# The gate and up projections of a feed-forward stage, with seven products of half blocks in the place of eight

## The chip, the cores and the metric

The kernel runs on one core of one Trainium2 chip. The metric is the time of one execution on the device in microseconds; the time before is the median of three runs. TensorE (PE) multiplies matrices; its weight loads are listed apart as PEld. VectorE (DVE), ScalarE (ACT) and GpSimd (POOL) work element by element, and SyncE (SP) issues the transfers.

## The reference

A decoder trunk of two layers on 512 tokens of width 1024, in float32. The first layer mixes with a gated linear recurrence, the second with RWKV-7; each is followed by the same feed-forward block, and that is what the change touches:

```python
def _conv_ffn(x, norm, w_up, conv_w, conv_b, w_down):
    h = _rmsnorm(x, norm)
    u = jnp.einsum('btd,df->btf', h, w_up)                      # 1024 -> 2 * 3072
    gate = _causal_dwconv(u[..., :D_FF], conv_w, conv_b)        # 3 taps along the tokens
    hid = jax.nn.gelu(gate, approximate=True) * u[..., D_FF:]
    return jnp.einsum('btf,fd->btd', hid, w_down)               # 3072 -> 1024
```

## The kernel before

Channels lie on the 128 partitions and the 512 tokens along the free dimension. Activations are held as blocks of 128 channels; `D_FF` is 24 such blocks for the gate half of `w_up` and 24 for the up half.

**Three matmuls for a product.** Each float32 operand is split into a high part, rounded to the fast format fp32r, and the rest. `mm3` (L51 to L53) issues three matmuls for one product: high by high, high weight by low activation, low weight by high activation. A weight tile holds 1024 elements per partition; `split` (L90, L93) makes its high part on ACT (`wh`) and its low part on DVE (`wl`). `weights_load` fetches such a tile in one transfer of 512 KB, three tiles ahead, and `weights_split` runs two ahead. All these tiles, and the split inputs `xs`, share one pool of 21 buffers (`b4`).

**The feed-forward stage.** `gate_up(third)` makes eight gate blocks and eight up blocks, four at a time, each a sum over 8 blocks of input channels in one bank of PSUM. A gate block is scaled by the norm's factor `rb` (L581, into `gpad`), convolved over tokens (ACT L584, DVE L586 twice) and put through GELU (ACT L588). An up block is scaled (L592), multiplied by the gate (L593), and split into `hid` (L90, L93). `down(third, hid)` multiplies eight blocks of `hid` with `w_down` and adds the sums to the residual. In layer 0 the weights are stationary and the tokens move (L637 adds); in layer 1 the tokens are stationary (L625 to L627, L630), so that the result lies by tokens. The order is gate and up 0, gate and up 1, down 0, gate and up 2, down 1, down 2.

**What stands ahead.** The stage before ends with a projection whose evacuation (`fin`, L532 in layer 0) adds to the residual `x` and at once makes the split input of the feed-forward stage, block by block: `norm_block` (L284 to L291).

**The order.** A scheduler places the instructions of each engine at build time in the order of the program text, as far as it finds buffers and inputs ready by its own estimate, and puts in the waits. On the chip each engine runs its list strictly in that order.

## Time and profile before

| | |
|---|---|
| three runs | 1317.26, 1319.48, 1319.39 us; median 1319.39 us |
| the profiled execution | 1318.34 us, its span 1316.6 us |
| PE, PEld | 1296.2 us (98%), 1057.5 us (80%) |
| DVE, ACT, POOL | 842.1 us (64%), 609.2 us (46%), 72.5 us (6%) |
| granted TensorE clock | 0.998 |
| HBM | 114.44 MB read, 90 GB/s over the span |

The span is the stretch that the profile covers; the execution is 1.74 us longer. A group of the profile is named by line, engine, operation and tiles, with its busy time, the mean duration of one and the idle time just before. Matmuls are pipelined: a duration is longer than the distance from one start to the next, and that distance is the price of one. The same holds, by some 0.08 us, for DVE.

### The profile page before, as it was taken

Reading aid. Unit: us, or ns where it says so; the run is one execution under the profiler, and the core shown is the slowest. Engines: PE = TensorE matmul, PEld = TensorE weight load, DVE = VectorE, ACT = ScalarE, POOL = GpSimd, SP = SyncE. Lnnn points to the kernel's source line nnn. Section 1 sums busy time; section 2 is a strip of 40 time slices with the busy share of each in tenths; the row PEclk is TensorE's granted clock in tenths of the full one; section 3 lists DMA queues with packets and bytes.
Section 4 is the critical chain, followed back from the end, with each engine's and each line's share of the span. In section 5 each row is a group of like instructions: output and inputs, shape, how many; then the busy total and the mean of one; then the engine's idle time right before and its main releaser. Section 6 shows DMA issues by size and latency. Waiting matters only on the chain.

```text
span 1316.6 us, 20618 instructions
## 1 busy us (share of the span) xinstructions
PE 1296.2 (98%) x8547; PEld 1057.5 (80%) x8547; DVE 842.1 (64%) x1276; ACT 609.2 (46%) x964; POOL 72.5 (6%) x114
## 2 busy tenths in 40 slices
PE   9999999999999999999999999999999999999998
PEld 7877888888888888876678787778888888888886
DVE  5988756555436555587989975777564554365523
ACT  6897544233224423358844567655542332244311
POOL 4000000000000000021001121210000000000000
PEclk9999999999999999999999999999999999999999
DMA  6323333323233443213303112133333222334311
GB/s 194 116 64 97 96 112 96 96 64 96 97 96 96 128 116 109 95 37 95 108 25 97 43 53 83 43 97 96 97 96 96 64 96 96 96 96 128 113 63 64
DMA packets 72126, 120.30 MB, mean 91 GB/s; under 512 B 9498, under 2 KB 21476, under 8 KB 71904
## 3 DMA queue, kind: packets, MB, share of 16 engines
q1 hardware_dynamic: 70672, 117.20, 28.6%
q8 instruction: 67, 1.10, 0.3%
q10 hardware_dynamic: 576, 1.05, 0.2%
q0 software_dynamic: 784, 0.74, 0.2%
q14 instruction: 27, 0.22, 0.1%
HBM read 114.44 MB, written 4.52 MB: 90 GB/s over the span
## 4 chain that ended last, share of the span: by engine, by line
PE 85%; DVE 8%; ACT 5%; issue 1%; DMA 0%; SPq 0%; POOLq 0%; POOL 0%; DVEq 0%; ACTq 0%
PE acc L51 22%; PE acc L53 22%; PE acc L52 21%; PE acc L626 3%; PE acc L625 3%; PE acc L627 3%; DVE X L1053 1%; DVE wl L93 1%; DVE DA L1051 1%; PE s L1171 1%; ACT L483 1%; PE pd L1253 1%; ACT L472 0%; PE py L1264 0%; PE pe L1215 0%
## 5 line engine op out<-in xcount | busy, mean ns | idle before, releaser
L51 PE MATMUL acc<-xs,wh 128*128 128x512 f32 x896 | 350.2, 392 | 0.3 <-ACT wh L90 0.3
L53 PE MATMUL acc<-xs,wl 128*128 128x512 f32 x896 | 348.3, 390 | 1.4 <-DVE wl L93 1.4
L93 DVE TENSOR_TENSOR wl<-raw,wh 128x1024 fp32r<-128x1024 f32 (+1 forms) x201 | 242.8, 1216 | 166.1 <-PE acc L52 94.8
L52 PE MATMUL acc<-xs,wh 128*128 128x512 f32 x896 | 348.8, 389 | 0.0
L90 ACT CAST wh<-raw 128x1024 fp32r<-128x1024 f32 (+1 forms) x201 | 207.9, 1045 | 259.2 <-DVE wl L93 169.8
L53 PEld LDWEIGHTS acc<-xs,wl 128*128 128x128 f32 x896 | 168.2, 188 | 37.7 <-DVE wl L93 2.2
L51 PEld LDWEIGHTS acc<-xs,wh 128*128 128x128 f32 x896 | 168.1, 188 | 35.4 <-ACT wh L90 0.8
L52 PEld LDWEIGHTS acc<-xs,wh 128*128 128x128 f32 x896 | 168.3, 188 | 34.4
L586 DVE SCALAR_TENSOR_TENSOR cv<-gpad,pv,cv 128x512 f32<-128x512 f32 x96 | 71.9, 749 | 22.1 <-ACT cv L584 21.0
L90 ACT CAST hid<-un 128x512 fp32r<-128x512 f32 x48 | 29.8, 620 | 108.6 <-DVE un L593 108.6
L626 PE MATMUL acc<-wh,hid 128*128 128x512 f32 (+1 forms) x200 | 76.8, 384 | 0.0
L625 PE MATMUL acc<-wh,hid 128*128 128x512 f32 (+1 forms) x200 | 76.5, 382 | 0.0
L627 PE MATMUL acc<-wl,hid 128*128 128x512 f32 (+1 forms) x200 | 75.9, 380 | 0.0
L52 PE MATMUL acc<-hid,wh 128*128 128x512 f32 x192 | 75.7, 394 | 0.0
L53 PE MATMUL acc<-hid,wl 128*128 128x512 f32 x192 | 75.6, 394 | 0.0
L51 PE MATMUL acc<-hid,wh 128*128 128x512 f32 x192 | 75.5, 393 | 0.0
L592 DVE TENSOR_TENSOR un<-acc,rb 128x512 f32<-128x512 f32 x48 | 33.1, 689 | 44.3 <-PE acc L53 44.3
L93 DVE TENSOR_TENSOR hid<-un,hid 128x512 fp32r<-128x512 f32 x48 | 33.2, 691 | 31.1 <-ACT hid L90 31.1
L584 ACT ACTIVATE cv<-gpad,pv 128x512 f32<-128x512 f32 x48 | 39.2, 817 | 20.7 <-DVE gpad L581 20.5
L588 ACT ACTIVATE ge<-cv 128x512 f32<-128x512 f32 x48 | 30.1, 627 | 35.9 <-DVE cv L586 35.9
L630 DVE TENSOR_TENSOR xtok<-xtok,acc 128x512 f32<-128x512 f32 (+1 forms) x25 | 16.6, 666 | 45.5 <-PE acc L627 45.5
L625 PEld LDWEIGHTS acc<-wh,hid 128*128 128x128 f32 x200 | 37.5, 188 | 8.0
(424 smaller groups left out, 2165.8 us busy)
## 6 DMA issues: line engine op xcount, KB each, us to landing
raw<-in_ffn_w_up_dram SPq DMA_DIRECT2D x96, 512.0 KB, 3.8
raw<-in_ffn_w_down_dram SPq DMA_DIRECT2D x48, 512.0 KB, 3.7
raw<-in_rwkv_w_rkv_dram SPq DMA_DIRECT2D x24, 512.0 KB, 3.9
raw<-in_lru_w_in_dram SPq DMA_DIRECT2D x16, 512.0 KB, 3.9
raw<-in_lru_w_out_dram SPq DMA_DIRECT2D x8, 512.0 KB, 3.9
raw<-in_rwkv_w_out_dram SPq DMA_DIRECT2D x8, 512.0 KB, 3.6
xd<-x SPq DMA_DIRECT2D x8, 256.0 KB, 2.0
AR<-xd SPq DMA_DIRECT2D x1, 2048.0 KB, 7.9
```

The costliest lines, as they stand in the source:

```text
L51: nc.tensor.matmul(ps, wh, xh, start=start, stop=False)
L52: nc.tensor.matmul(ps, wh, xl, start=False, stop=False)
L53: nc.tensor.matmul(ps, wl, xh, start=False, stop=stop)
L90: put = (self.nc.vector.tensor_copy if dve else self.nc.scalar.copy)(hi, src)
L93: self.nc.vector.tensor_tensor(lo, src, hi.bitcast(F32), ALU.subtract)
L584: nc.scalar.activation(cv, gp[:, 0:T], AF.Identity, bias=self.vec(f"ffn_conv_b{l}", fb), scale=cw(0))
L586: nc.vector.scalar_tensor_tensor(cv, gp[:, j : j + T], cw(j), cv, ALU.mult, ALU.add)
L588: nc.scalar.activation(ges[o], cv, AF.Gelu_apprx_tanh)
L592: nc.vector.tensor_tensor(un, ps, rbs[0], ALU.mult)
L625: nc.tensor.matmul(ps, hh[:, s], wh[:, k, m], start=kk == 0, stop=False)
L626: nc.tensor.matmul(ps, hl[:, s], wh[:, k, m], start=False, stop=False)
L627: nc.tensor.matmul(ps, hh[:, s], wl[:, k, m], start=False, stop=kk == 7)
```

## The change

Only the feed-forward stages change. For each pair of blocks the gate half and the up half of `w_up` (1024 rows by 256 columns each) and the input (1024 channels by 512 tokens) are cut in two along the 1024 summed channels; the tokens are cut in two as well. The result is then a two by two matrix of blocks (gate and up, first and last 256 tokens), and seven products of half blocks, each 512 channels deep and 256 tokens wide, stand for eight (Winograd's form of Strassen's way). The price is paid in sums:

- of the inputs, once a stage (`operands`): differences and sums `xt_1479` to `xt_1482`, 12 of them on DVE and 16 splits, 128x256 each; a new `norm_part` makes the first of them while the stage before is evacuated;
- of the weights, once a pair (`Pair.weights`): four sums of 1024 elements per partition on POOL (`S1`, `S2`, `S4`, and one in place), and seven splits where four tiles needed four;
- of the products: three accumulate in a common bank, others are added by DVE or copied by ACT (`s`); the scaling by `rb` moves to POOL for half of the gate and for the finished gate `ge`.

The twelve pairs of a layer are consumed by `down` in four calls of four blocks and one of eight. The order of products is the list `seq`; `ahead` splits weights two products ahead. The number and size of weight transfers stay: 512 KB, 96 for `w_up` and 48 for `w_down`; those of `w_up` now hold four rows of blocks by 256 columns.

```diff
+            def gu(six):
+                for c in range(six * 512, six * 512 + 512, 256):
+                    self.quads.append(len(plan))
+                    for half, r in ((1, 0), (0, 0), (0, 512), (1, 512)):
+                        add(up, r, half * DFF + c, 4, True)
+            def dd(row, n):
                 for g in range(2):
-                    for k in range(0, 8, 2):
-                        add(dn, third * 1024 + k * P, g * 512)
+                    for k in range(0, n, 2):
+                        add(dn, row + k * P, g * 512)
 
             gu(0)
-            gu(1)
-            dd(0)
-            gu(2)
-            dd(1)
-            dd(2)
+            for six in range(1, 6):
+                gu(six)
+                if six < 5:
+                    dd((six - 1) * 512, 4)
+            dd(2048, 8)
...
+    def norm_part(self, b, gain):
+        if b >= KB // 2:
+            return self.norm_block(b, gain)
+        nc = self.nc
+        if b % 2 == 0:
+            self.halves = self.b4(F32R, (2, 2, T // 2), f"xs{b}"), self.b4(F32, (2, 2, T // 2), f"xd{b}")
+        v, d = (t[:, b % 2] for t in self.halves)
+        xb = self.x[:, b, :]
+        nc.scalar.mul(v[:, 0], xb[:, 0 : T // 2], gain)
+        nc.vector.scalar_tensor_tensor(v[:, 1], xb[:, 0 : T // 2], gain, v[:, 0].bitcast(F32), ALU.mult, ALU.subtract)
+        self.squares(b)
+        nc.scalar.mul(d[:, 0], xb[:, T // 2 :], gain)
+        nc.vector.scalar_tensor_tensor(d[:, 1], xb[:, 0 : T // 2], gain, d[:, 0], ALU.mult, ALU.subtract)
+        return v[:, 0], v[:, 1], d[:, 0], d[:, 1]
...
+            def operands():
+                n1, t2, t3, t4 = sums
+                def parts(t, k, f):
+                    nc.scalar.copy(t[:, 0, k], f)
+                    nc.vector.tensor_tensor(t[:, 1, k], f, t[:, 0, k].bitcast(F32), ALU.subtract)
+                for k in range(4):
+                    parts(n1, k, xs[k][3])
+                stt, f = nc.vector.scalar_tensor_tensor, {}
+                for k in range(4):
+                    xb = self.x[:, 4 + k, :]
+                    f[k] = two(t("s", 7))
+                    t2f, t4f = f[k][:, 0], f[k][:, 1]
+                    stt(t2f, xb[:, H:], gain(4 + k), xs[k][3], ALU.mult, ALU.add)
+                    parts(t2, k, t2f)
+                    stt(t4f, xb[:, 0:H], gain(4 + k), t2f, ALU.mult, ALU.subtract)
+                for k in range(4):
+                    if k % 2 == 0:
+                        t3f = two(t("s", 7))
+                    stt(t3f[:, k % 2], self.x[:, 4 + k, H:], gain(4 + k), xs[k][2], ALU.mult, ALU.subtract)
+                    parts(t3, k, t3f[:, k % 2])
+                for k in range(4):
+                    parts(t4, k, f[k][:, 1])
+                op = {1: [xs[k][:2] for k in range(4)]}
+                op[2], op[3] = ([tuple(part[:, h] for part in xs[4 + k]) for k in range(4)] for h in (slice(0, H), slice(H, T)))
+                for i, v in ((5, n1), (6, t2), (7, t3), (4, t4)):
+                    op[i] = [(v[:, 0, k], v[:, 1, k]) for k in range(4)]
+                return op
+            op = operands()
...
+            class Pair:
+                def __init__(pair, n):
+                    i = quads[n]
+                    self.weights_load(i + 4)
+                    pair.n, pair.gp = n, gpads[n % 2]
+                    a11, a21, a22, a12 = (self.loaded.pop(i + j) for j in range(4))
+                    pair.f = {1: a11, 7: a21, 4: a22, 2: a12}
+                    pair.w, pair.bank, pair.s = {}, {}, {}
+                def weights(pair, p):
+                    f = pair.f
+                    if p == 1:
+                        f[5], f[6] = self.b4(F32, (4, 256), "S1"), self.b4(F32, (4, 256), "S2")
+                        gt(f[5], f[7], f[4], ALU.add)
+                        gt(f[6], f[5], f[1], ALU.subtract)
+                        gt(f[7], f[1], f[7], ALU.subtract)
+                    if p == 5:
+                        f[3] = self.b4(F32, (4, 256), "S4")
+                        gt(f[3], f[6], f[2], ALU.subtract)
+                    hi, lo = self.b4(F32R, (4, 256), f"hi{p}"), self.b4(F32R, (4, 256), f"lo{p}")
+                    nc.scalar.copy(hi, f[p])
+                    tt(lo, f[p], hi.bitcast(F32), ALU.subtract)
+                    pair.w[p] = hi, lo
+                def product(pair, p):
+                    name = {1: "A", 5: "F", 2: "D"}.get(p)
+                    if name:
+                        pair.bank[name] = two(self.bank("acc" + name))
+                    ps = pair.bank[name or {3: "F"}.get(p, "A")]
+                    hi, lo = pair.w.pop(p)
+                    for e in range(2):
+                        c = slice(e * P, e * P + P)
+                        for k in range(4):
+                            self.mm3(ps[:, e], (hi[:, k, c], lo[:, k, c]), op[p][k], bool(name) and e + k == 0, e + k == 4, more=not name)
+                        self.background(0.5)
+                    s, bank, gp = pair.s, pair.bank, pair.gp
+                    if p in (1, 6, 7):
+                        s[p] = two(t("s", 7))
+                        nc.scalar.copy(s[p], bank["A"])
+                    if p == 2:
+                        tt(s[1], s[1], bank["D"], ALU.add)
+                    if p == 7:
+                        tt(gp[:, :, 2 + H :], s[7], bank["F"], ALU.subtract)
+                        gt(gp[:, :, 2 + H :], gp[:, :, 2 + H :], rb(H, T), ALU.mult)
+                    if p == 4:
+                        tt(gp[:, :, 2 : 2 + H], bank["A"], rb(0, H), ALU.mult)
+                        pair.gate()
+                    if p == 3:
+                        tt(s[6], s[6], bank["F"], ALU.subtract)
+                        pair.up()
+                def gate(pair):
...
+                    gt(ge, ge, rb(0, T), ALU.mult)
+                def up(pair):
+                    hid = hidden(pair.n)
+                    for i, h in ((1, slice(0, H)), (6, slice(H, T))):
+                        x = pair.s[i]
+                        tt(x, x, pair.ge[:, :, h], ALU.mult)
+                        nc.scalar.copy(hid[:, :, 0, h], x)
+                        tt(hid[:, :, 1, h], x, hid[:, :, 0, h].bitcast(F32), ALU.subtract)
+                    hids.extend((hid[:, e, 0], hid[:, e, 1]) for e in range(2))
...
+            seq = []
+            for n in range(12):
+                if n in (0, 1, 2, 3):
+                    seq += [(n, 1)] + ([(n - 1, 4), (n - 1, 3)] if n else [])
+                elif n % 2:
+                    seq += [(n, 1), (n - 1, 4), (n - 1, 3)]
+                else:
+                    seq += [(n, 1)]
+                seq += [(n, p) for p in (5, 6, 2, 7)]
+                if n % 2 and n > 1:
+                    seq += [(n, 4), (n, 3)]
+            made, at = [0], [0]
+            def ahead(j):
+                while made[0] < min(j, len(seq)):
+                    n, p = seq[made[0]]
+                    if n not in pairs:
+                        pairs[n] = Pair(n)
+                    pairs[n].weights(p)
+                    made[0] += 1
+            def products(upto, more=2):
+                while True:
+                    n, p = seq[at[0]]
+                    at[0] += 1
+                    ahead(at[0] + more)
+                    pairs[n].product(p)
+                    if p == 1 and n < 11:
+                        self.weights_load(quads[n + 1] + 4 if quads[n + 1] == quads[n] + 4 else quads[n] + 6)
+                    if n == 0 and p in (5, 2):
+                        start(int(p == 2))
+                    if p == 7:
+                        self.weights_split(quads[n] + 6)
+                    if (n, p) == upto:
+                        return
...
+            for n in range(3, 12, 2):
+                products((n, 7))
+                if n == 11 and not last:
+                    self.norm_begin()
+                    self.push(self.lora_weights())
+                down(n, 2 * n - 6, 4 if n < 11 else 8, lambda: products((n, 3)), lambda: ahead(at[0] + 2))
```

The lists of the engines change with it. Names ending in a number are tiles of the built program; `raw` is a loaded weight tile, `wh`/`wl` and `hi`/`lo` its high and low parts, `x_68` the residual, and `xd` a part of an input that `norm_part` has made. First DVE, where the stage before layer 0's feed-forward ends (its last evacuation is the first row). Before:

```order
L532 SCALAR_TENSOR_TENSOR x_68<-acc3_1318,pv_78,x_68 128x512
L285 SCALAR_TENSOR_TENSOR xs7_1461<-x_68,pv_78,xs7_1461 128x512
L291 TENSOR_TENSOR sqacc_1144<-sqacc_1144,sq_1464 128x512
L93 TENSOR_TENSOR wl25_1482<-raw25_1385,wh25_1481 128x1024
L93 TENSOR_TENSOR wl26_1521<-raw26_1479,wh26_1520 128x1024
L301 TENSOR_SCALAR ms_1514<-ssq_1509 128x4
L93 TENSOR_TENSOR wl27_1558<-raw27_1518,wh27_1557 128x1024
L93 TENSOR_TENSOR wl28_1564<-raw28_1555,wh28_1563 128x1024
```

Now:

```order
L562 SCALAR_TENSOR_TENSOR x_68<-acc3_1326,pv_78,x_68 128x512
L622 TENSOR_TENSOR xt_1479<-xd0_1255,xt_1479 128x256 x2
L622 TENSOR_TENSOR xt_1479<-xd2_1295,xt_1479 128x256
L293 SCALAR_TENSOR_TENSOR xs7_1465<-x_68,pv_78,xs7_1465 128x512
L304 TENSOR_TENSOR sqacc_1144<-sqacc_1144,sq_1468 128x512
L622 TENSOR_TENSOR xt_1479<-xd2_1295,xt_1479 128x256
L631 SCALAR_TENSOR_TENSOR s_1491<-x_68,pv_78,xd0_1255 128x256
L631 SCALAR_TENSOR_TENSOR s_1496<-x_68,pv_78,xd0_1255 128x256
L633 SCALAR_TENSOR_TENSOR s_1491<-x_68,pv_78,s_1491 128x256
L622 TENSOR_TENSOR xt_1480<-s_1491,xt_1480 128x256
```

And, after fifteen more rows of the same kinds:

```order
L622 TENSOR_TENSOR xt_1482<-s_1506,xt_1482 128x256
L684 TENSOR_TENSOR lo1_1543<-raw24_1387,hi1_1542 128x1024
L684 TENSOR_TENSOR lo5_1549<-S1_1537,hi5_1548 128x1024
L684 TENSOR_TENSOR lo6_1553<-S2_1538,hi6_1552 128x1024
```

Before, the low part that the first product needs (`wl24_1388`) is made ahead of these rows, and the next one stands fourth in them. Now the first, `lo1_1543`, stands behind the 28 operations of `operands` (L622, L631, L633, L637). At the same place PE has, before:

```order
L53 MATMUL acc3_1318<-out_1208,wl23_1382 128x512
L51 MATMUL acc0_1475<-xs0_1254,wh24_1387 128x512
L52 MATMUL acc0_1475<-xs0_1254,wh24_1387 128x512
L53 MATMUL acc0_1475<-xs0_1254,wl24_1388 128x512
L51 MATMUL acc0_1475<-xs1_1271,wh24_1387 128x512
L52 MATMUL acc0_1475<-xs1_1271,wh24_1387 128x512
L53 MATMUL acc0_1475<-xs1_1271,wl24_1388 128x512
```

and now:

```order
L51 MATMUL acc3_1326<-out_1208,wl23_1390 128x512
L51 MATMUL accA_1556<-xs0_1254,hi1_1542 128x256 x2
L51 MATMUL accF_1595<-xt_1479,hi5_1548 128x256
L51 MATMUL accA_1556<-xs0_1254,lo1_1543 128x256
L51 MATMUL accA_1556<-xs0_1254,hi1_1542 128x256 x2
L51 MATMUL accA_1556<-xs0_1254,lo1_1543 128x256
L51 MATMUL accA_1556<-xs2_1294,hi1_1542 128x256 x2
L51 MATMUL accA_1556<-xs2_1294,lo1_1543 128x256
```

The fourth of the new matmuls needs `lo1_1543`, the first weight's low part; what follows it in the list needs it too. Next POOL through the first pairs of layer 0. Before there was nothing there but small work between the stages:

```order
L424 MEMSET graw_484 128x1024
L307 TENSOR_TENSOR rs_1516<-ms_1514,mhalf_76 128x4
L307 TENSOR_TENSOR rs_4184<-ms_4182,mhalf_76 128x4
L890 MEMSET selk_4352 128x256
L898 COPY selk_4352<-pv_78 64x1 x16
```

Now, with L676 to L681 the sums of weights, L706 and L724 the scaling:

```order
L681 TENSOR_TENSOR S4_1546<-S2_1538,raw27_1535 128x1024
L676 TENSOR_TENSOR S1_1659<-raw29_1585,raw30_1587 128x1024
L337 TENSOR_TENSOR rs_1627<-ms_1625,mhalf_76 128x4
L677 TENSOR_TENSOR S2_1660<-S1_1659,raw28_1583 128x1024
L678 TENSOR_TENSOR raw29_1585<-raw28_1583,raw29_1585 128x1024
L706 TENSOR_TENSOR gpad0_1475<-gpad0_1475,rb_1699 128x2x256
L681 TENSOR_TENSOR S4_1772<-S2_1660,raw31_1589 128x1024
L724 TENSOR_TENSOR ge_1803<-ge_1803,rb_1699 128x1024
L676 TENSOR_TENSOR S1_1910<-raw33_1766,raw34_1768 128x1024
```

Each pair has four sums and two scalings in this list. Last DVE in the second pair's products. Before, evacuation of up blocks and splits of weights stood in turn:

```order
L592 TENSOR_TENSOR un_2031<-acc0_1943,rb_1553 128x512
L593 TENSOR_TENSOR un_2031<-un_2031,ge_1884 128x512
L93 TENSOR_TENSOR hid_2034<-un_2031,hid_2034 128x512
L592 TENSOR_TENSOR un_2049<-acc1_1944,rb_1553 128x512
L593 TENSOR_TENSOR un_2049<-un_2049,ge_1903 128x512
L93 TENSOR_TENSOR hid_2052<-un_2049,hid_2052 128x512
L592 TENSOR_TENSOR un_2067<-acc2_1945,rb_1553 128x512
L593 TENSOR_TENSOR un_2067<-un_2067,ge_1922 128x512
L93 TENSOR_TENSOR wl43_2158<-raw43_2125,wh43_2157 128x1024
L93 TENSOR_TENSOR hid_2070<-un_2067,hid_2070 128x512
```

Now:

```order
L708 TENSOR_TENSOR gpad0_1475<-accA_1556,rb_1699 128x2x256
L684 TENSOR_TENSOR lo6_1816<-S2_1660,hi6_1815 128x1024
L722 SCALAR_TENSOR_TENSOR cv_1804<-gpad0_1475,pv_78,cv_1804 128x512
L722 SCALAR_TENSOR_TENSOR cv_1809<-gpad0_1475,pv_78,cv_1809 128x512
L722 SCALAR_TENSOR_TENSOR cv_1804<-gpad0_1475,pv_78,cv_1804 128x512
L722 SCALAR_TENSOR_TENSOR cv_1809<-gpad0_1475,pv_78,cv_1809 128x512
L711 TENSOR_TENSOR s_1657<-s_1657,accF_1595 128x512
L684 TENSOR_TENSOR lo2_1852<-raw31_1589,hi2_1851 128x1024
L730 TENSOR_TENSOR s_1581<-s_1581,ge_1803 128x512
L730 TENSOR_TENSOR s_1657<-s_1657,ge_1803 128x512
L684 TENSOR_TENSOR lo7_1881<-raw29_1585,hi7_1880 128x1024
L732 TENSOR_TENSOR hid_1844<-s_1581,hid_1844 128x2x256
```

The multiplication by the finished gate (L730) stands ahead of the split of the pair's product 7 (`lo7_1881`), and `ge` comes from POOL's L724. The scheduler also gives each split a buffer; `lo5_1775` in front of these rows waits for the end of product 4 of the pair before, whose buffer it takes, and POOL's `S1_1659` for the end of product 5 of its predecessor.

More of the change, by code (lines that the diff above doesn't have):

```diff
@@ L547, in ffn @@
             rbs, norm = [], []
-            gpads = [pool.tile([P, T + 2], F32, name=f"gpad{i}") for i in range(2)]
+            gpads = [pool.tile([P, 2, T + 2], F32, name=f"gpad{i}") for i in range(2)]
             for u in gpads:
-                nc.vector.memset(u[:, 0:2], 0.0)
+                nc.vector.memset(u[:, :, 0:2], 0.0)
+            late = []
             xtok = None
@@ L571, in start @@
                         self.push(by_tokens())
-            def gate_up(third):
-                hid = []
-                for sub in range(2):
-                    ges = {}
-                    def gate(o, ps):
-                        fb = third * 8 + sub * 4 + o
-                        gp = gpads[fb % 2]
-                        nc.vector.tensor_tensor(gp[:, 2:], ps, rbs[0], ALU.mult)
+            H = T // 2
+            two = lambda ps: ps.rearrange("p (e t) -> p e t", e=2)
+            sums = [pool.tile([P, 2, 4, H], F32R, tag="xt", name="xt", bufs=4) for _ in range(4)]
@@ new lines, in ffn, with hidden @@
+            op = operands()
+            def hidden(n):
+                if last and n // 2 % 2:
+                    if n == 2:
+                        self.drain()
+                    if n % 2 == 0:
+                        self.xhid = self.const.tile([P, 2, 2, 2, T], F32R, tag="x", name="hid", bufs=1)
+                    return self.xhid[:, n % 2]
+                return pool.tile([P, 2, 2, T], F32R, tag="hid", name="hid", bufs=2 if last else 4)
+            rb = lambda u, v: rbs[0][:, u:v].unsqueeze(1).to_broadcast([P, 2, v - u])
@@ new lines, in ffn @@
+            tt, gt = nc.vector.tensor_tensor, nc.gpsimd.tensor_tensor
+            class Pair:
[47 more added lines that the diff above has]
+                def gate(pair):
+                    ge = pair.ge = pool.tile([P, 2, T], F32, tag="ge", name="ge", bufs=2)
+                    for e in range(2):
+                        fb = 2 * pair.n + e
@@ L602, in gate_up @@
-                    self.project(xs, gate, after=None if rbs else start, rate=0.5)
-                    self.project(xs, up, rate=0.5)
-                return hid
-            def down(third, hid):
-                final = third == 2
+                            nc.vector.scalar_tensor_tensor(cv, pair.gp[:, e, j : j + T], cw(j), cv, ALU.mult, ALU.add)
+                        nc.scalar.activation(ge[:, e], cv, AF.Gelu_apprx_tanh)
+                    gt(ge, ge, rb(0, T), ALU.mult)
[7 more added lines that the diff above has]
+                    hids.extend((hid[:, e, 0], hid[:, e, 1]) for e in range(2))
@@ L608, in down @@
+            def down(n, b0, blocks, between, then):
+                final = n == 11
+                pieces = blocks // 2
                 for g in range(2):
```

115 lines of the change are left out of this document (53 added, 62 removed).

## The prediction

> **What bounds the kernel now.** I read the page first: how busy the engines are, and who stands on the chain that ended last.
>
> ```profile
> PE 1296.2 (98%) x8547; PEld 1057.5 (80%) x8547; DVE 842.1 (64%) x1276; ACT 609.2 (46%) x964; POOL 72.5 (6%) x114
> PE 85%; DVE 8%; ACT 5%; issue 1%; DMA 0%; SPq 0%; POOLq 0%; POOL 0%; DVEq 0%; ACTq 0%
> ```
>
> PE carries the time. The share over the span says little of the two stages that change, so next the busy time of each engine in these two stretches (span, then busy time and count for PE, PEld, DVE, ACT, POOL; then granted clock, DMA share and rate):
>
> ```profile
> 158.19:555.29 397.10, 397.10 (x1745) 325.86 (x1744) 220.71 (x276) 137.52 (x166) 1.94 (x1) 1.00 0.33 101
> 911.37:1310.16 398.79, 398.79 (x1801) 330.45 (x1799) 207.15 (x263) 134.34 (x171) 4.24 (x5) 1.00 0.30 94
> ```
>
> PE is never idle in either. So every matmul saved there is time saved, until another engine is late; DVE has 44% and 48% of the two free, POOL almost all.
>
> What a matmul costs is the distance of starts, from PE's timeline: the last 30 of 512 columns, the 48 of 256 columns behind them, and 42 of 256 columns elsewhere.
>
> ```profile
> 1297.64 0.39 PE L625 MATMUL acc<-wh,hid 128*128 128x512 f32 x1
> ...
> 1304.28 0.39 PE L627 MATMUL acc<-wl,hid 128*128 128x512 f32 x1
> 1304.50 0.28 PE L625 MATMUL acc<-wh,hid 128*128 128x256 f32 x1
> ...
> 1310.04 0.28 PE L627 MATMUL acc<-wl,hid 128*128 128x256 f32 x1
> 700.87 0.28 PE L999 MATMUL acc<-wh,mix 128*128 128x256 f32 x1
> ...
> 705.78 0.28 PE L1001 MATMUL acc<-wl,mix 128*128 128x256 f32 x1
> ```
>
> 6.64 us over 29 steps is 0.229 us; 5.54 over 47 is 0.118 and 4.91 over 41 is 0.120, each with a weight load of its own. I take 0.119.
>
> **The matmuls.** Gate and up of a layer are now 48 blocks by 8 by 3 = 1152 matmuls of 512 columns, 263.8 us. They become 12 pairs by 7 products by 24 = 2016 of 256 columns: 239.9 us (237.7 to 241.5). `down` keeps its 576. Gain 23.9 us a layer, all of it on the path.
>
> **DVE and POOL.** Their prices: distances of starts in DVE's timeline, mean durations by shape, and POOL's one wide operation with its least, median and greatest.
>
> ```profile
> 158.12 0.69 DVE L291 TENSOR_TENSOR sqacc<-sqacc,sq 128x512 f32<-128x512 f32 x1
> 158.72 0.75 DVE L532 SCALAR_TENSOR_TENSOR x<-acc,pv,x 128x512 f32<-128x512 f32 x1
> 161.73 2.36 DVE L93 TENSOR_TENSOR wl<-raw,wh 128x1024 fp32r<-128x1024 f32 x2
> 164.70 3.50 DVE L93 TENSOR_TENSOR wl<-raw,wh 128x1024 fp32r<-128x1024 f32 x3
> L586 DVE SCALAR_TENSOR_TENSOR cv<-gpad,pv,cv 128x512 f32<-128x512 f32 x96 | 71.9, 749 | 22.1 <-ACT cv L584 21.0
> L1260 DVE TENSOR_TENSOR tu<-pd,decay 64x256 f32<-64x256 f32 x28 | 11.8, 421 | 17.2 <-PE pd L1253 16.9
> L1285 POOL TENSOR_TENSOR bv<-x,bon x8: 1037/1044/1367, 763.2 to 868.5; 128x512 f32<-128x512 f32 x8
> ```
>
> A split of 1024 elements costs DVE 1.14 us (3.50 less 2.36), 512 elements 0.60, with two operations 0.66 (0.749 less the overlap of about 0.08), 256 elements 0.34 to 0.42 (I take 0.36). POOL needs 1.04 us for 512 elements of two inputs, so a sum of 1024 is an estimate of 2.0, between 1.04 (were it all start-up) and 2.1.
>
> A pair then costs DVE 7 splits, 4 convolutions, 4 operations that read PSUM and 4 on the hidden half: 8.0 + 2.6 + 2.4 + 2.4 = 15.4 us. POOL's four sums and two scalings cost 5 x 2.0 + 1.0 = 11.0. PE needs 7 x 24 x 0.119 = 20.0. Side by side, PE would still be last. But they don't run side by side:
>
> ```profile
> 763.18 1.04 POOL L1285 TENSOR_TENSOR bv<-x,bon 128x512 f32<-128x512 f32 x1
> 763.40 1.37 DVE L1280 SCALAR_TENSOR_TENSOR ytok<-mu,ytok 128x512 f32<-128x512 f32 x1
> 840.99 0.68 DVE L1292 TENSOR_TENSOR ytok<-ytok,lnw 128x512 f32<-128x512 f32 x1
> 841.21 1.37 POOL L1285 TENSOR_TENSOR bv<-x,bon 128x512 f32<-128x512 f32 x1 [3.10 <-DVE BK L93]
> 841.71 1.42 DVE L1293 TENSOR_TENSOR ytok<-ytok,bv 128x512 f32<-128x512 f32 x1
> 805.92 1.29 DVE L1178 TENSOR_TENSOR W<-s,masks 128x512 f32<-128x512 f32 x2 [0.81 <-PE s L1171]
> 806.06 1.64 POOL L1288 TENSOR_TENSOR mu<-var,mhalf 128x8 f32<-128x8 f32 x1
> ```
>
> POOL's operation lasts to 764.22, and DVE's, begun inside it, ends 0.55 us behind that, 0.7 late; at 841 POOL waits 0.33 for DVE, then DVE 0.74 for POOL. Two operations that read PSUM, at 805.92, are not held (1.29 for two). So DVE's work on two SBUF inputs and POOL's are one queue: 13.0 + 11.0 = 24.0 us a pair, 26.4 if nothing overlaps, against PE's 20.0.
>
> The Trainium skill, "SBUF — State Buffer", section "SBUF: two separate sides", says the same of every such operation: the two engines share a port pair, whichever starts first keeps it for its whole instruction, and DVE takes part when both its inputs lie in SBUF. The rows agree in both cases; by it the sum below stands, without it its second term would be 14.
>
> **Up to the first `down`.** In the order now, DVE does after its last evacuation (158.72, PE's first matmul of the stage is at 158.19) 28 operations of `operands` and two of the norm before `lo1`: 0.75 + 28 x 0.36 + 0.67 + 0.60 + 1.14 = 13.2 us to 171.9. PE has 3 matmuls in that time, so it stands about 13 us (11 to 16) in each layer. What is queued behind on PE is everything. Then 26 products lead to the first `down`: 74.3 us on PE. DVE's list in this stretch has 28 x 0.36, 30 splits 34.2, 13 PSUM reads 7.8, 12 convolutions 7.9, 12 others 7.2, 2.0 for the evacuation and norm: 69.2 us. POOL has 13 sums, 3 small and 3 wide scalings: 35. One queue gives 104, less at most 8.5 for the PSUM reads: 95.7. I take 101, near the upper end, since L730 waits for POOL's `ge` with `lo7` behind it. Against 74.3 that is +27 (21 to 33), the 13 included.
>
> The granted clock: the first 14 transposes of the program took 3.25 us, the next 20 only 2.35.
>
> ```profile
> 1.44 3.25 PE L342 MATMUL warm<-ident 128*128 128x128 f32 x14 [1.44 <-POOL ident masks.py:199]
> 5.26 2.35 PE L342 MATMUL lnps<-ident 128*128 128x128 f32 x20
> ```
>
> After 13 us idle I expect such a start again: +1 us (0 to 2, 14 x 0.115 being 1.6). The Trainium skill, "TensorE: Matmul & The Clock Gate", section "Part 1: The HAM clock gate", has half the clock after an idle window of 3.4 us, for about as long; by it this term is an estimate of 1.7. No run here shows such a wait in the middle.
>
> **Between the `down` calls.** Two pairs and a `down` of four blocks: PE 40.0 + 96 x 0.229 = 62.0 us. DVE has 18 splits, 8 convolutions and 24 of 0.60: 40.2; POOL 22.0. One queue without overlap is 62.2: equal. Lists in strict order lose something: 0 to 5 us for each of four, I take 2.5: +10 a layer. The last `down`, 44 us on PE, has only 8 splits beside it: 0.
>
> **Hidden or level.** The groups of splits (high part on ACT, low part on DVE: busy, mean ns | idle before) and of weight loads, and the transfers (count, size, us to landing):
>
> ```profile
> L90 ACT CAST wh<-raw 128x1024 fp32r<-128x1024 f32 (+1 forms) x201 | 207.9, 1045 | 259.2 <-DVE wl L93 169.8
> L93 DVE TENSOR_TENSOR wl<-raw,wh 128x1024 fp32r<-128x1024 f32 (+1 forms) x201 | 242.8, 1216 | 166.1 <-PE acc L52 94.8
> L53 PEld LDWEIGHTS acc<-xs,wl 128*128 128x128 f32 x896 | 168.2, 188 | 37.7 <-DVE wl L93 2.2
> raw<-in_ffn_w_up_dram SPq DMA_DIRECT2D x96, 512.0 KB, 3.8
> ```
>
> ACT gets 36 more casts a layer at 1.05 us and 36 copies: some 60 us beside 137 busy of 397, hidden by PE; if not, by DVE, which needs the cast first. Transfers are the same number and size on SP's queue; they land in 3.8 us. They now wait for buffers: 13 of 21 are free for weights. Nothing (0 to 2) for it, since a tile is asked for one pair ahead.
>
> **Sum.** A layer: -23.9 + 27 + 1 + 10 = +14; two layers +28. The profiled execution is 1318.34 us, 1.05 below the median of 1319.39. On the median: 1347. With all terms at their good ends (-26 + 21 + 0 + 0) it is 1309, at their bad ends (-22 + 33 + 2 + 20) 1385.
>
> **Rivals.**
> - *POOL's sums slip into DVE's gaps and hold nothing up* (chance 0.24, the other side). For it: DVE alone (69.2) stays below PE's 74.3 and POOL runs ahead where buffers are free. Against: 763.40 and 841.71. Then only the 14 us at the start are lost: 2 x (-23.9 + 14) = -20, 1300. It decides where the stretch to the first `down`, beyond the idle start, costs under 10 us.
> - *Strict order costs every pair* (0.12): `lo7` behind L730, behind POOL, behind ACT's GELU, 4 us in each of 12 pairs and no better elsewhere: -23.9 + 14 + 48 = +38 a layer, 1395.
> - *A half product doesn't run at 0.119* (0.05): operands read at a stride, or weight loads of 188 ns showing through. At 0.13, 2016 x 0.011 = 22 us more a layer on PE: the gain is gone, and with +38 for the rest (27 + 1 + 10) 2 x 36 = +72: 1391. Against: the 48 matmuls at 0.118.
> - *The start doesn't stall* (0.04): 2 x -23.9, 1271.
>
> **Chances.** The forecast has 0.55. Within 0.2% (1316.8 to 1322.0, about what these three runs could tell from no change) 0.05; faster 0.24 + 0.04 and 0.02 of the forecast's low end: 0.30; slower 0.65. The range 1296 to 1390 takes in the gap rival and leaves out the fourth and half of the second and third. The forecast's own is 1309 to 1385.
>
> **What would show it.** The chain of waits should name DVE `lo` (L684) and POOL ahead of PE; PE's idle time should stand at 158 to 172 and again behind 911; POOL's sums near 2.0 us or longer, DVE's splits well over their 1.22 in the mean; 256-column matmuls 0.118 to 0.120 apart. If DVE's splits stay at 1.22 beside POOL, or PE is busy from 172 on, I am wrong.

## The result, and the profile after

The changed kernel takes 1473.57 us (median of four runs, 1472.25 to 1475.10) against 1319.22 before: a ratio of 1.117, 95% interval 1.1155 to 1.1193. The forecast was slower, 1347 us; it is 154 us slower and not 28.

The page of the changed kernel, engines and chain:

```profile
PE 1307.5 (89%) x10275; PEld 1137.3 (77%) x10275; DVE 1090.7 (74%) x1444; ACT 721.1 (49%) x1148; POOL 443.5 (30%) x258
PE 53%; DVE 26%; issue 7%; ACT 7%; POOL 6%; DVEq 0%; POOLq 0%; ACTq 0%
PE acc L51 19%; PE accA L51 12%; DVE lo L684 7%; DVE cv L722 4%; POOL ge L724 3%; PE accF L51 3%; PE acc L798 3%; PE acc L797 2%; PE acc L796 2%; POOL raw L678 2%; PE accD L51 2%; DVE wl L94 2%; DVE s L730 1%; PE lg L51 1%; DVE X L1239 1%
```

PE has fallen from 98% to 89% of a longer span, and the chain that ended last now goes through DVE (26%), ACT (7%) and POOL (6%). Layer 0's feed-forward stage, cut where its first matmul of each `down` starts (span, then busy time and count of PE, PEld, DVE, ACT, POOL; granted clock, DMA share, rate):

```profile
158.61:275.00 116.39, 83.89 (x641) 81.74 (x641) 91.61 (x104) 55.64 (x80) 49.38 (x20) 0.84 0.20 64
275.00:351.84 76.84, 66.22 (x434) 59.94 (x433) 55.65 (x52) 28.93 (x36) 32.55 (x12) 0.91 0.27 89
351.84:426.62 74.78, 66.00 (x433) 59.74 (x433) 52.20 (x50) 28.93 (x36) 31.74 (x12) 0.93 0.26 84
426.62:502.17 75.55, 67.08 (x434) 61.20 (x433) 51.76 (x51) 28.92 (x36) 31.75 (x12) 0.91 0.27 86
502.17:577.58 75.41, 66.21 (x433) 59.88 (x433) 51.35 (x48) 28.62 (x36) 30.35 (x12) 0.93 0.30 92
577.58:634.04 56.46, 52.42 (x242) 42.57 (x241) 41.37 (x54) 24.56 (x34) 5.12 (x2) 0.97 0.33 108
```

The stage takes 475.4 us where it took 397.1; layer 1's (996.42 to 1464.08) takes 467.7 where it took 398.8. The other 6 us stand in the stage between them, which takes 362.4 in place of 356.1 and was not taken apart. In no stretch is any engine always busy: in the four middle ones PE works 66 of 75 us, DVE 52, POOL 32. DVE's and POOL's busy times together are 84 us of 75, and they contain each other's waits. This is how it looks in DVE's and POOL's timelines in the second pair:

```profile
207.88 1.21 DVE L684 TENSOR_TENSOR lo<-raw,hi 128x1024 fp32r<-128x1024 f32 x1
211.40 5.57 DVE L730 TENSOR_TENSOR s<-s,ge 128x512 f32<-128x512 f32 x2 [2.31 <-POOL ge L724]
216.90 3.37 DVE L684 TENSOR_TENSOR lo<-raw,hi 128x1024 fp32r<-128x1024 f32 x1
220.19 1.28 DVE L732 TENSOR_TENSOR hid<-s,hid 128x512 fp32r<-128x512 f32 x2
208.10 3.27 POOL L724 TENSOR_TENSOR ge<-ge,rb 128x1024 f32<-128x1024 f32 x1 [6.21 <-ACT ge L723]
211.32 2.35 POOL L676 TENSOR_TENSOR S<-raw,raw 128x1024 f32<-128x1024 f32 x1
213.75 2.67 POOL L677 TENSOR_TENSOR S<-S,raw 128x1024 f32<-128x1024 f32 x1
216.39 2.80 POOL L678 TENSOR_TENSOR raw<-raw,raw 128x1024 f32<-128x1024 f32 x1
```

From 211.3 to 219.2 POOL runs three sums back to back. DVE's two L730, 1.28 us for two where POOL is still (so L732 at 220.19), take 5.57: 2.8 us each, one for each POOL operation. The split behind them takes 3.37 in place of 1.21. The wait goes the other way too: L724 begins at 208.10, inside DVE's split, and its 3.27 us are 0.9 of waiting and 2.4 of work. The groups of the page say the same in the mean (busy, mean ns | idle before):

```profile
L684 DVE TENSOR_TENSOR lo<-raw,hi 128x1024 fp32r<-128x1024 f32 x96 | 172.1, 1795 | 74.5 <-PE accA L51 38.0
L676 POOL TENSOR_TENSOR S<-raw,raw 128x1024 f32<-128x1024 f32 x24 | 57.6, 2398 | 353.7 <-PE accF L51 183.0
L724 POOL TENSOR_TENSOR ge<-ge,rb 128x1024 f32<-128x1024 f32 x24 | 76.7, 3196 | 140.8 <-ACT ge L723 140.8
L722 DVE SCALAR_TENSOR_TENSOR cv<-gpad,pv,cv 128x512 f32<-128x512 f32 x96 | 102.7, 1109 | 9.0 <-ACT cv L720 8.7
```

PE's waits follow from that: the copy of bank A (ACT L701) stands in ACT's list behind the cast of the hidden half, the cast waits for L730, and L730 for POOL. Rows of PE's timeline: the start, then the first such wait, then (earlier in time) a product at full clock.

```profile
169.27 0.80 PE L51 MATMUL accA<-xs,hi 128*128 128x256 f32 x2 [10.50 <-ACT hi L683]
175.52 0.58 PE L51 MATMUL accF<-xt,hi 128*128 128x256 f32 x1 [5.46 <-ACT hi L683]
177.00 0.58 PE L51 MATMUL accA<-xs,lo 128*128 128x256 f32 x1 [0.90 <-DVE lo L684]
177.38 0.63 PE L51 MATMUL accA<-xs,hi 128*128 128x256 f32 x2
...
181.01 0.41 PE L51 MATMUL accA<-xs,lo 128*128 128x256 f32 x1
...
218.16 0.79 PE L51 MATMUL accA<-xt,hi 128*128 128x256 f32 x2 [6.12 <-ACT s L701]
...
188.08 0.40 PE L51 MATMUL accD<-xs,hi 128*128 128x256 f32 x2
...
190.83 0.28 PE L51 MATMUL accD<-xs,lo 128*128 128x256 f32 x1
```

The product at 188.08 runs 23 steps in 2.75 us, 0.120 each: the half products cost what was forecast. Behind the start, 17 steps from 177.38 take 3.63 us, 0.214 each: the clock is at half (0.50 in the slices from 172 to 180).

### The profile page after: what moved, and what is told of

It is laid out like the page before. It is cut to its first block, busy times and chain, and to the rows that moved or that the text cites. A ratio compares the mean times of both kernels' runs of the same rounds, so it can differ in the third digit from the quotient of the medians.

```text
span 1470.5 us, 24747 instructions
## 1 busy us (share of the span) xinstructions
PE 1307.5 (89%) x10275; PEld 1137.3 (77%) x10275; DVE 1090.7 (74%) x1444; ACT 721.1 (49%) x1148; POOL 443.5 (30%) x258
## 4 chain that ended last, share of the span: by engine, by line
PE 53%; DVE 26%; issue 7%; ACT 7%; POOL 6%; DVEq 0%; POOLq 0%; ACTq 0%
PE acc L51 19%; PE accA L51 12%; DVE lo L684 7%; DVE cv L722 4%; POOL ge L724 3%; PE accF L51 3%; PE acc L798 3%; PE acc L797 2%; PE acc L796 2%; POOL raw L678 2%; PE accD L51 2%; DVE wl L94 2%; DVE s L730 1%; PE lg L51 1%; DVE X L1239 1%
## 5 line engine op out<-in xcount | busy, mean ns | idle before, releaser
L51 PE MATMUL accA<-xt,hi 128*128 128x256 f32 x1152 | 223.2, 296 | 50.3 <-ACT s L701 50.3
L51 PEld LDWEIGHTS accA<-xt,hi 128*128 128x128 f32 x1152 | 191.5, 205 | 54.0 <-ACT s L701 53.2
L684 DVE TENSOR_TENSOR lo<-raw,hi 128x1024 fp32r<-128x1024 f32 x96 | 172.1, 1795 | 74.5 <-PE accA L51 38.0
L51 PE MATMUL accA<-xt,lo 128*128 128x256 f32 x576 | 169.9, 295 | 5.5 <-DVE lo L684 5.5
L676 POOL TENSOR_TENSOR S<-raw,raw 128x1024 f32<-128x1024 f32 x24 | 57.6, 2398 | 353.7 <-PE accF L51 183.0
L683 ACT CAST hi<-raw 128x1024 fp32r<-128x1024 f32 x96 | 100.1, 1047 | 94.1 <-PE acc L798 31.9
L94 DVE TENSOR_TENSOR wl<-raw,wh 128x1024 fp32r<-128x1024 f32 (+1 forms) x105 | 127.2, 1218 | 16.7 <-ACT wh L91 12.9
L51 PEld LDWEIGHTS accA<-xt,lo 128*128 128x128 f32 x576 | 118.1, 205 | 6.6 <-DVE lo L684 6.6
L684 DVE TENSOR_TENSOR lo<-S,hi 128x1024 fp32r<-128x1024 f32 x72 | 105.0, 1460 | 21.8 <-PE accA L51 12.4
L91 ACT CAST wh<-raw 128x1024 fp32r<-128x1024 f32 (+1 forms) x105 | 107.2, 1037 | 27.0 <-issue 14.7
L724 POOL TENSOR_TENSOR ge<-ge,rb 128x1024 f32<-128x1024 f32 x24 | 76.7, 3196 | 140.8 <-ACT ge L723 140.8
L51 PEld LDWEIGHTS acc<-hid,wh 128*128 128x128 f32 x384 | 77.0, 204 | 36.0 <-ACT wh L91 18.6
L701 ACT COPY s<-accA 128x512 f32<-128x512 f32 x72 | 42.1, 585 | 104.5 <-PE accA L51 104.5
L798 PE MATMUL acc<-wl,hid 128*128 128x512 f32 (+1 forms) x200 | 78.8, 404 | 13.2 <-DVE wl L94 13.2
L730 DVE TENSOR_TENSOR s<-s,ge 128x512 f32<-128x512 f32 x48 | 48.4, 1047 | 54.6 <-POOL ge L724 54.6
```

The source lines that it names most:

```text
L51: mm = lambda *a, **kw: self.nc.tensor.matmul(ps, *a, skip_group_check=more, **kw)
L91: put = (self.nc.vector.tensor_copy if dve else self.nc.scalar.copy)(hi, src)
L94: self.nc.vector.tensor_tensor(lo, src, hi.bitcast(F32), ALU.subtract)
L676: gt(f[5], f[7], f[4], ALU.add)
L683: nc.scalar.copy(hi, f[p])
L684: tt(lo, f[p], hi.bitcast(F32), ALU.subtract)
```

## The experiments

Theory A: DVE and POOL are one queue, and its length holds PE up. Theory B: the lists in strict order do, whatever the operations cost. A third suspect was the slow clock behind each wait. Beside each run stands one of the kernel before on the same chip (1317.3 to 1320.0 us). All kernels of this section but the last two ran once, so a difference of 2 or 3 us between two of them says nothing.

**Work moved from POOL to DVE.** DVE needs 1.14 us where POOL needs 2.40 by itself, so each operation moved shortens the common queue by 1.26. The first kernel has the last line of the diff, the second the four sums, the third all of it and L706.

```diff
-                        gt(f[5], f[7], f[4], ALU.add)
-                        gt(f[6], f[5], f[1], ALU.subtract)
+                        tt(f[5], f[7], f[4], ALU.add)
+                        tt(f[6], f[5], f[1], ALU.subtract)
...
-                    gt(ge, ge, rb(0, T), ALU.mult)
+                    tt(ge, ge, rb(0, T), ALU.mult)
```

> The scaling of the finished gate (L724) moves from POOL (3.25 us where DVE stands still) to DVE (about 1.2). Theory A (POOL and DVE are one queue, its length sets the time): 24 x 2.05 = 49 us less and some 10 us of lost clock with it, about 1415. Theory B (the load doesn't matter, the strict order of gate, multiplication, cast and copy does): the chain shortens by 2.05 us only where it is the last, at 14 gaps of PE, 29 us, about 1445.

> The four sums of weights of a pair (L676 to L681) move from POOL to DVE; the scalings stay on POOL. Theory A: POOL's 10.2 us a pair leave the queue and 4.6 come to DVE, 5.6 x 24 = 134 us less, of which PE's own time lets about 100 through: 1370. Theory B: the wait for the finished gate stays with its gaps of 3.4 us, and DVE's list is longer: 1430 or more.

> Sums and both scalings move to DVE, POOL does nothing in the two stages. DVE then has about 53 us of work for each 61 us of PE. Theory A: PE is last again but for the starts (17 us idle and 2 of clock each): 1315 to 1330. Theory B: a gap of 1 to 3 us with its slow clock stays in each pair: 1370. If DVE's list in strict order is worse than POOL beside it: over 1400.

Measured: 1436.98, 1395.43 and 1367.44 us: 37, 78 and 106 less than the changed kernel. By queue length it would be 24 x 1.26 = 30 for the first (37 came) and 96 x 1.26 = 121 for the second (78 came; its four middle stretches still take 66.0 to 68.9 us, with PE waiting in each, and what keeps the rest is not shown). The expectations had POOL's price too high and so both theories' numbers off; e1 fell nearer to B, e2 between, e3 on B's 1370. Putting more work on the busier engine made the kernel faster each time; but 106 of 154 us is not all.

**The start alone.** The first splits ahead of the sums of inputs (`ahead(2)` in front of `operands()`); then 125 idle matmuls in PE's list at each start.

> The splits of the first two products are asked for ahead of the sums of the inputs; nothing else. If the idle start is a cost of its own: up to 9 us less in each layer, 1455. If the queue of DVE and POOL up to the first down product sets the time, the start is only idle time moved: 1468 to 1474.

> 125 matmuls that do nothing, on inputs that are ready, stand in PE's list at each start (80 ahead of the first product, 45 ahead of the rest of it), so that PE isn't idle while it waits for the first splits; 125 x 0.119 = 14.9 us in 17 us of waiting. If the slow clock after the idle time costs on the path: 24 matmuls at 0.119 in place of 0.213, 2 x 2.2 us less, 1469. If the queue of DVE and POOL sets the time behind it: 1473. If the fillers are themselves late: up to 1480.

1470.03 and 1477.90 us. In the first, the product at the start comes 6.6 us earlier (its low part at 170.39 in place of 177.00), and the wait that stood at 295.53 stands at 293.06: most of it is waited elsewhere. With the queue as long as it is, the idle start is hardly a cost of its own. In the second PE is busy through most of the start, and nothing is won; but a wait of 3.41 us is left ahead of 176.43, and behind it the clock is at 0.54 up to 180. So this run did not take the slow clock away, and what that costs is not shown by it.

**The order alone.** `pair.up()` is put off to behind product 6.

> The multiplication by the gate and the split of the hidden half are asked for two products later, behind the copy of product 6, so that the copy of a bank and the splits of weights don't stand behind the wait for POOL's scaling. Theory B (strict order): the gaps of 3.4 us ahead of product 7 go, 8 x 3.4, and part of the early ones, with their slow clock: 1430. Theory A (one queue): the work is the same, 1465 to 1475.

1464.65 us, 9 less: theory A's side. The 6.12 us at 218 shrink to 2.02, and waits for splits (2.43 at 220) take part of their place.

**Is it the length of POOL's operations?** Three kernels: sums made but not read, no sums, and unread sums of 32 elements in place of 1024 with every instruction, wait and buffer kept. All three leave the sums out of their products. The lower half of the diff is in all three, the upper in the last.

```diff
-                        gt(f[5], f[7], f[4], ALU.add)
+                        q = lambda i: f[i][:, :, 0:8]; gt(q(5), q(7), q(4), ALU.add)
...
-                    nc.scalar.copy(hi, f[p])
-                    tt(lo, f[p], hi.bitcast(F32), ALU.subtract)
+                    src = f[{5: 7, 6: 1, 3: 2}.get(p, p)]; nc.scalar.copy(hi, src)
+                    tt(lo, src, hi.bitcast(F32), ALU.subtract)
```

> POOL makes its four sums as before, but nothing reads them: the splits take loaded tiles (the sums are left out of the products). Theory A1 (a DVE operation on two SBUF inputs can't run beside a POOL sum, whoever needs it): hardly faster, 1445 to 1470. Theory A2 (the splits wait for POOL's results): as without the sums, about 1380.

> No sums of weights at all, on any engine (left out of the products); both scalings stay on POOL. With the sums on DVE it was 1395, with 109 us more work for DVE than here: 1365 to 1390. The distance to the kernel with the unread sums is the price of the shared queue (theory A1: some 70 us; A2: under 15).

> As the kernel with the unread sums, with every POOL instruction, buffer and wait kept, but each sum over 32 elements per partition in place of 1024 (left out of the products). If the length of POOL's operations beside DVE is the cost: 1334 to 1350. If the buffers and waits that come with the sums are: 1470 to 1490.

1487.56, 1333.81 and 1338.28 us. Nothing reads the result of the unread sums, and yet they cost as much as the whole loss; made short, they cost 4 us. The expectations had the second kernel too slow (1365 to 1390) and its distance from the first too small (70 us; it is 154). The engines' busy times, DVE's convolutions and POOL's first sum, in the kernel with unread sums and then in that with short ones:

```profile
PE 1304.4 (88%) x10275; PEld 1136.8 (77%) x10275; DVE 1082.5 (73%) x1444; ACT 719.2 (48%) x1148; POOL 426.8 (29%) x258
L722 DVE SCALAR_TENSOR_TENSOR cv<-gpad,pv,cv 128x512 f32<-128x512 f32 x96 | 112.8, 1234 | 1.0 <-ACT cv L720 1.0
L676 POOL TENSOR_TENSOR S<-raw,raw 128x1024 f32<-128x1024 f32 x24 | 58.6, 2442 | 382.6 <-DVE lo L684 157.3 <-PE acc L51 130.1 <-PE accF L51 68.3
```

```profile
PE 1261.7 (94%) x10275; PEld 1104.1 (83%) x10275; DVE 964.1 (72%) x1444; ACT 721.6 (54%) x1148; POOL 201.1 (15%) x258
L722 DVE SCALAR_TENSOR_TENSOR cv<-gpad,pv,cv 128x512 f32<-128x512 f32 x96 | 65.7, 745 | 1.0 <-ACT cv L720 1.0
L676 POOL TENSOR_TENSOR S<-raw,raw 128x32 f32<-128x32 f32 x24 | 7.0, 292 | 382.8 <-DMA raw<-in_ffn_w_up_dram 151.9 <-DVE lo L684 127.9 <-PE accF L51 84.4
```

The same 96 convolutions take 112.8 us beside long sums and 65.7 beside short ones, and DVE's 1444 operations 118 us more in all: they are held while they run. DVE's splits also wait for POOL to give back a tile, though nothing reads the sums, but that changes little: 82.9 us with long sums, 58.1 with short ones. So it is the length of POOL's operations beside DVE, and mostly the hold, that costs: this is shown. With 96 sums of about 2.4 us, 230 us of POOL's work, the 154 us over the kernel without sums are 0.67 us of the kernel for each us of POOL.

In the kernel with short sums the four middle stretches take 64.4, 64.9, 64.0 and 64.0 us; PE is busy for 247.9 of the 257.3, at a granted clock of 1.00. In the changed kernel it is busy for 265.5 of 302.6, at 0.91 to 0.93. So 18 of the 45 us are the same matmuls at a slower clock behind the waits, and the rest is waiting. What the waits alone would cost at full clock was not tried.

**Does it help to cut POOL's operations small?** Pieces of 256 elements, so that DVE gets its turn sooner.

> Each POOL operation on weights and gates is cut into pieces of 256 elements (four for a sum, two for the scaling of the half gate), about 0.62 us each; the sums and their readers are the same. If the two engines take turns operation by operation and DVE's work is what is late: a DVE operation waits 0.6 us and not 2.4 to 2.8, 1380 to 1410. If only the summed length of the one queue counts: 1470 to 1500, since each piece adds its start.

1469.64 us: nothing is won, as the second expectation has it. A piece that isn't held costs 0.71 to 0.75 us, four of them more than the 2.40 of one whole. DVE is held for less (busy 1032.0 us in place of 1090.7) and POOL for longer (573.5 in place of 443.5). By the added length alone the kernel should have become slower; whether the shorter turns made up for that is not shown.

**Towards a better kernel.** All sums on DVE, in place and just ahead of their splits; the first weight's parts made while the stage before is evacuated; product 2 of pair 0 second; `up` later.

```diff
+                    if p == 5:
+                        f[5] = f[6] = f[3] = self.b4(F32, (4, 256), "S1")
+                        tt(f[5], f[7], f[4], ALU.add)
+                    if p in (6, 7, 3):
+                        o, a, b = {6: (6, 5, 1), 7: (7, 1, 7), 3: (3, 6, 2)}[p]
+                        tt(f[o], f[a], f[b], ALU.subtract)
...
-                seq += [(n, p) for p in (5, 6, 2, 7)]
+                seq += [(n, p) for p in ((5, 6, 2, 7) if n else (2, 5, 6, 7))]
...
-                    pairs[n].product(p)
+                    pairs[n].product(p); (p == 6 or (n, p) == (11, 3)) and late and late.pop()()
```

> All sums and scalings on DVE, each sum made in place just ahead of its split; the first weight's parts are made while the stage before is evacuated; pair 0 runs product 2 second, which needs no sums of inputs; the multiplication by the gate stands two products later. Against 1367 with POOL empty: the starts lose 16 us of idle time and 2 of clock each, of which about 12 a layer can be won: 1343; with the gaps ahead of product 7 and in the first pairs, 1320 to 1345. If DVE's total is the bound in the first stretch (94 us of its work beside 74 of PE's), little: 1355.

> As the one before, with splits three products ahead in place of two. If the chain sum, cast, split is late for PE at single products: 5 to 15 us less than that kernel; if DVE's load or the buffers are the bound: within 4 us of it.

1345.41 us: 22 less than with POOL merely empty, at the upper end of what was expected. With splits three ahead it is 1351.25, where a gain or no change was expected. Now PE is busy for 232.0 of the 233 us from 282 to 515, in the middle of the stage, and the loss is at its ends. There the `down` products were moved one pair earlier, the next stage's work beside the last one was put behind its first half, the last `down` was cut into one of two blocks and one of six, and products without sums were put first:

```diff
-            for n in range(3, 12, 2):
+            for n in (2, 4, 6, 8, 11):
...
-                    self.push(self.lora_weights())
...
+            seq = [(0, 1), (0, 2), (1, 1), (1, 2)] + [(0, p) for p in (5, 6, 7, 4, 3)] + [(1, p) for p in (5, 6, 7)] + [q for q in seq if q[0] > 1 or q[0] == 1 and q[1] in (4, 3)]
```

> As e13_best, with the down products one pair earlier (behind pairs 2, 4, 6, 8 and 11, the transfers in that order): DVE has one pair less to do ahead of the first one. If DVE's bunched work holds the first stretch: 2 x 8 to 12 us less, 1325. If single waits do: 1340 to 1350.

> As e14_early_down, and the background work of the next stage (made beside the last down product of layer 0, where PE waited 9.8 us) starts later. If that work was ahead of the splits in DVE's and ACT's lists: 5 to 9 us less than e14_early_down. If the wait only moves into the next stage: the same.

> As e14_push, with a down product of two blocks behind pair 10 and one of six at the end in place of one of eight. PE waited some 5 us in each layer beside pairs 9 to 11. If DVE's bunched work is the reason: 1323 to 1330; if the extra evacuations (8 a layer at 0.68 us) eat it: 1335.

> As e16_even_end, and products 1 and 2 of pairs 0 and 1, which need no sums of inputs and no sums of weights, run first: 5.7 us more of PE's work beside the 28 operations. If the start is DVE's load ahead of the first such product: 2 x 4 to 6 us less than e16_even_end, 1315 to 1322. If the split parts of two pairs crowd the buffers: the same or worse.

> As e14_push, with products 1 and 2 of pairs 0 and 1 first. The same step gave 7.7 us with the other down products (1343.6 to 1335.9): 1327 against 1335; DVE's load at the start is then part of the rest. If 1333 to 1337, it isn't. Faster than before only if both starts come to nothing, which the list does not suggest.

> As e17_start, with 30 matmuls that do nothing ahead of product 2 and 12 ahead of pair 1, where PE waited 3.1 and 1.1 us. If the slow clock behind these waits costs: 2 to 4 us a layer less than e17_start, since PE is now last most of the time. If DVE's list holds PE there anyway: within 2 us of it or up to 3 above.

Measured: 1346.15 (no gain from the earlier `down` alone), 1335.08 (11 less, where 5 to 9 were expected), 1343.55 (the evened end is worse, a miss), 1335.86 (1315 to 1322 was expected, a miss too), and as medians of four runs 1329.88 (ratio to before 1.0083, interval 1.0068 to 1.0098) and 1332.92 (1.0110, interval 1.0093 to 1.0127). Starting with products that need no sums is worth 5 to 8 us; filling the waits is worth nothing again (from 164.7 to 170 the clock rises from 0.50 to 1.00, but from 180 to 236 it falls from 1.00 to 0.94). The best version is still 0.8% slower than the kernel before. Its layer 0, the start to the first `down`, a short stretch, the middle, and the end up to the next stage's first matmuls:

```profile
158.60:236.00 77.40, 64.97 (x496) 61.72 (x495) 70.82 (x99) 40.78 (x62) 3.06 (x1) 0.96 0.25 82
236.00:254.00 18.00, 16.53 (x85) 13.49 (x84) 13.27 (x16) 6.67 (x8) 0.00 (x0) 1.00 0.36 117
254.00:480.00 226.00, 225.04 (x1600) 208.51 (x1598) 194.51 (x224) 105.51 (x130) 0.00 (x0) 1.00 0.32 103
480.00:550.00 70.00, 65.94 (x392) 57.61 (x390) 58.57 (x74) 33.67 (x45) 0.00 (x0) 0.98 0.32 100
```

In the middle PE works 225.0 of 226 us at full clock, and two pairs with a `down` take 62 us, as forecast for PE alone. In the first stretch DVE is busy 70.8 of 77.4 us and PE 65.0: the sums of inputs are bunched there. How the rest of the 58 us over PE's own 1271 (1319 less 48) divides between the two ends and the next stage, where the put-off work goes, was not taken apart.

## Why the prediction was wrong

The sign and the mechanism were right, and the signs named for it showed: DVE's `lo` and POOL stand in the chain (though PE leads it with 53%), PE waits at 158 to 177, sums take over 2.0 us, splits of loaded tiles 1.80 in the mean, half products 0.114 to 0.120. The size was not, and the time lies 84 us above the range. With what layer 0 measured, the forecast's sum for it is -23.9 + 42 + 55 + 7 = +80 in place of +14 (the stage grew by 78): the start with its clock, the middle, and an end that was put at nothing.

- *The matmuls, -23.9 a layer:* right. 0.120 us a half product, and PE 62 us for two pairs and a `down` once nothing holds it up.
- *Between the `down` calls, +10 a layer: the step that failed.* It set DVE's 40.2 and POOL's 22.0 beside PE's 62.0, found them equal and took 2.5 us a stretch. The four took 302.6 us, not 258: +55 over PE's 248 in layer 0 and not +10. The kernel with short sums has 257.3 there. So some 2.5 us is what a stretch loses with next to no sums in the queue, and the shared queue, which the forecast had in the sum but without a cost, is worth 11.3 us a stretch.
- *The price of a POOL operation in it:* 2.0 us was taken from the 1.04 of a 512-element one; by itself it is 2.40 (1.19 for 512 in L706's least). That is 13.2 us a pair and not 11.0, so the queue is 66.6 us and not 62.2, above PE's. The Trainium skill, "GPSIMD Engine Reference", section 3.1, has 4497 ns for an add of 2048 elements; half of it, an estimate of 2.25, would have pointed there, and this measured more.
- *What that leaves:* 75.6 less 66.6 is 9 us a stretch in which the queue stands still as well. POOL's L724 waits for ACT's GELU (43.9 us in the four stretches) and DVE's L708 for a bank (27.8), but how the 9 us divide was not taken apart. "Equal load" was read as "just enough"; that at equal load each wait in a strict list is added is argued from this, not shown by a run of its own.
- *Up to the first `down`, 101 + 1:* 116.4, 14 more, of the same cause: 97.8 with short sums. The idle start itself was 16.9 us where 13 was forecast; DVE's last evacuations were already held by the first sums (an operation of 0.69 us took 2.85 at 158.09).
- *The last `down`, 0:* its stretch took 56.5 us, 7 more than the 49.7 of PE's own (192 x 0.229 and two products of 24 x 0.119). PE waits there for the cast and the split of a `w_down` tile (3.34 us at 597.87, 0.70 at 602.20). With short sums it is still 54.6, so this is mostly not the queue with POOL.
- *The clock, +1:* some 2 us at the start (24 x 0.214 less 0.120), and the clock is 0.91 to 0.93 in the middle stretches, which the forecast left out. There PE's own work took 18 us longer than in the kernel with short sums; the fillers stood at the start alone and do not show what that costs.
- *Rivals.* That POOL's work slips into gaps (0.24) is refuted by the unread sums; its 1300 would need the sums to be free, and even without them it is 1334. Strict order costing every pair (0.12) had the nearest time, 1395, but by luck: undoing the order that it named gave 9 us.

The Trainium skill, "SBUF — State Buffer", section "SBUF: two separate sides", has the loser of the shared port pair block fully for a whole instruction. The rows at 211 to 219 agree: 2.8 us for a DVE operation of 0.66 between POOL's of 2.4. The rule was cited and its sum made; what it does to a list that is nearly full was not.

## What to carry to other kernels

Work put on POOL beside a DVE that has operations on two SBUF inputs isn't parallel work: here each us of it cost 0.67 us, and DVE did the same sum in half the time. When two engines are one queue, add their times, with the price of each operation at its own size, and ask for a clear margin below the engine that is to stay last; here 66.6 us of queue beside 62 of PE became a stretch of 75.6. To tell contention from dependence, keep the operation and drop its reader, then keep the instruction and make it short.

## What was not expected of the hardware

- POOL waits for DVE as DVE for POOL: L724's 3.27 us at 208.10 are 2.4 of work behind a split that had begun; its mean is 3.196.
- A POOL operation of 256 elements takes 0.71 to 0.75 us and one of 1024 takes 2.40: cutting it in four adds a fifth to its length.
- Behind two waits of the same 3.36 us the clock falls at different times. Behind the one at 496.88, three matmuls take 0.64 us at once. Behind the one at 347.47 they take 0.35 at first (347.93 to 348.28), and 0.64 only from 348.64 on:

```profile
347.47 0.50 PE L51 MATMUL accA<-xt,hi 128*128 128x256 f32 x2 [3.36 <-ACT s L701]
...
347.93 0.40 PE L51 MATMUL accA<-xt,hi 128*128 128x256 f32 x2
...
348.28 0.40 PE L51 MATMUL accA<-xt,hi 128*128 128x256 f32 x2
...
348.64 0.63 PE L51 MATMUL accA<-xt,hi 128*128 128x256 f32 x2
...
349.28 0.63 PE L51 MATMUL accA<-xt,hi 128*128 128x256 f32 x2
...
496.88 0.80 PE L51 MATMUL accA<-xt,hi 128*128 128x256 f32 x2 [3.36 <-ACT s L701]
...
497.69 0.63 PE L51 MATMUL accA<-xt,hi 128*128 128x256 f32 x2
...
498.33 0.63 PE L51 MATMUL accA<-xt,hi 128*128 128x256 f32 x2
```
